# Stick-breaking weights: TensorE's transposes replaced by VectorE's block transposes and a reorder through DRAM, with all heads in one list

## The chip, the cores and the metric

The kernel runs on one core of a Trainium2 chip. The metric is the device time of one execution in microseconds. Before the change it is 520.65 us (median of 3 runs, 520.26 to 520.73). The traces are of one execution taken by the hardware profiler.

## What is computed

One decoder layer over 1,024 tokens of width 1,024. An RMS norm is followed by an input projection into eight parts; three groups (a causal pooling mixer, stick-breaking attention, softmax attention into 256 memory tokens) each get a SiLU gate, and an output projection with a residual follows. The change is in the stick-breaking group, which has 8 heads of width 64:

```python
z = jnp.einsum('bqhd,bkhd->bhqk', qb, kb) * scale      # 128 queries, all keys up to them
mask = s_idx[None, :] < t_idx[:, None]
log_beta = jax.nn.log_sigmoid(z)
log_1m_beta = jnp.where(mask, jax.nn.log_sigmoid(-z), 0.0)
cum = jnp.cumsum(log_1m_beta, axis=-1)
log_a = log_beta + cum[..., -1:] - cum
a = jnp.where(mask, jnp.exp(log_a), 0.0)
out = jnp.einsum('bhqk,bkhd->bqhd', a, vb)
```

All inputs are float32. The kernel keeps that precision by splitting an operand of TensorE into a high part (rounded to the format that TensorE reads) and a low part (what the rounding left), and by adding up the products of the parts.

## The kernel before, in words

The hidden state lies transposed in SBUF as eight high and eight low tiles (`hh`, `hl`). A *unit* of the input projection makes 128 output columns for all tokens, in two halves of 512; a half is eight *steps* of three matmuls of 128x512 (L219, L222). A unit's weights are loaded by SP into the one buffer `wr` (L150), copied to the high part by ScalarE (L161) and subtracted to the low part by GpSimd in four pieces (L165). They are asked for one unit ahead. `u_q`, `u_k`, `u_v`, `u_g` are the units of the stick-breaking heads, two heads (a *pair*) in each; there are four pairs.

The weights `a` are not made by logarithms. `sb_main` takes the sigmoid of minus z (ScalarE, L668) into a tile `be` of 128 queries by L keys, and one scan on VectorE (L672) multiplies these up from the newest key to the oldest. The weights are the differences of neighbours in the scan's result. The kernel takes these differences on V's side instead: `v_unit` subtracts neighbouring rows of V, and the product of the scan's result less one with these differences is the output.

A *group* is one head h of a pair with one j of 0 to 3, that is two blocks of 128 queries (2j and 2j+1). A group has j+1 *chunks* of 256 keys. For each chunk TensorE transposes four 128x128 blocks of `be` (three in the last chunk, whose fourth lies above the diagonal) into PSUM (`a_t`, L517), ScalarE copies them, less one, to `ah` (L522), VectorE makes the low part `al` (L523), and TensorE multiplies V by both (`a_v`, L536). After the last chunk `av_out` adds the two halves of the accumulator, and the gate is multiplied on.

`v_unit` needs V with the tokens in the partitions. It does that already in the way that the change gives to the weights: VectorE transposes each 32x32 block of a 128x512 tile (L316), four DMAs write the blocks to DRAM in pieces of 128 bytes (L320), and two DMAs read them back (L324), after they have landed.

The order of TensorE's work is written by hand. `weave` puts the *main* list (scores, transposes and products of a pair) together with the *fill* list (steps of the projections), so that a main step comes when a simple model of the other engines (`occ`, `lat`) holds it ready. The other engines' orders follow from the order in which the program gives out the work and from what waits for what. All DMAs are issued by SP, one after the other: an issue that waits holds back those behind it. Four `be` tiles and two of each of `ah` and `al` are in turn. After the last pair, one more unit (`u_mg`) and the output projection (seven products, with sums of operands made on VectorE and GpSimd) follow.

## Time and profile before

| | |
|---|---|
| median of 3 runs | 520.65 us (520.26 to 520.73) |
| the profiled execution | 520.78 us, span 519.0 us |
| TensorE clock granted | 1.0 throughout |
| DMA queue of SP | 62,552 packets, 40.98 MB, 27.2% of the 16 engines' span |
| packets under 512 bytes | 27,334 |
| first and last scores of a stick-breaking head | 137.9 and 407.3 us |
| first matmul of the output projection | 438.3 us |

In a row of a group of instructions stand the line, the engine, the operation, what is written from what, the shape and the count; then the busy time in us and the mean in ns of one; then the engine's idle time ahead of them and what ended it. In the chain of waits a row is a start, the time that the piece adds to the end, the engine, the tile and the line. In the timeline a row is a start, a duration, and the instruction.

### The profile page before, as it was taken

The numbers are of one execution on the slowest core, as the hardware profiler recorded it, in microseconds if no ns is written. First come the engines' busy times: TensorE is split into PE (matmuls) and PEld (weight loads), VectorE is DVE, ScalarE is ACT, GpSimd is POOL, SyncE is SP. The second block draws the span as 40 slices with busy tenths as digits, with TensorE's granted clock in tenths as the row PEclk, the third lists the DMA queues.
The fourth block names the chain that finished last, engine by engine and source line by source line (L and its number), as shares of the span: only waits on it lengthen the run. The fifth ranks groups of instructions, "written<-read, shape, count | busy, mean of one in ns | idle before, by whom it ended". The sixth has DMA issues, their size and how long they took to land.

```text
span 519.0 us, 7552 instructions
## 1 busy us (share of the span) xinstructions
PE 506.7 (98%) x2692; PEld 426.1 (82%) x2692; DVE 391.2 (75%) x635; ACT 289.1 (56%) x562; POOL 177.8 (34%) x198
## 2 busy tenths in 40 slices
PE   7889999999999999999999999999999999999997
PEld 6668878888888888888888888888788888888886
DVE  4776776787597876887748776658987769999863
ACT  6887647677666654645455655444635549452400
POOL 4580334465222102202230221132527900045990
PEclk9999999999999999999999999999999999999999
DMA  8911021432311131023401133411010425504033
GB/s 301 352 43 42 3 80 40 104 81 56 88 40 42 42 81 42 1 81 81 101 21 42 42 85 69 92 42 33 9 40 11 153 72 173 169 33 163 0 122 122
DMA packets 62589, 41.45 MB, mean 80 GB/s; under 512 B 27334, under 2 KB 52184, under 8 KB 62552
## 3 DMA queue, kind: packets, MB, share of 16 engines
q1 hardware_dynamic: 62552, 40.98, 27.2%
q8 instruction: 21, 0.34, 0.3%
q14 instruction: 16, 0.13, 0.1%
HBM read 30.48 MB, written 6.29 MB: 71 GB/s over the span
## 4 chain that ended last, share of the span: by engine, by line
PE 88%; ACT 5%; DVE 4%; DMA 1%; issue 1%; SPq 0%; ACTq 0%
PE av L536 8%; PE z L664 7%; PE ta L517 6%; PE u_v L222 6%; PE u_q L222 6%; PE u_g L222 5%; PE u_k L222 5%; PE u_q L219 3%; PE u_v L219 3%; PE u_mg L222 3%; PE oS L1071 3%; PE oS L1073 3%; PE u_pv L222 3%; PE oS L1072 3%; PE u_g L219 3%; PE u_k L219 3%
## 5 line engine op out<-in xcount | busy, mean ns | idle before, releaser
L672 DVE TENSOR_TENSOR_SCAN be<-be,later 128x128 f32<-128x128 f32 (+3 forms) x64 | 92.7, 1462 | 11.9 <-ACT be L668 11.0
L522 ACT ACTIVATE ah<-ta,mone 128x512 fp32r<-128x512 f32 (+1 forms) x80 | 51.3, 644 | 48.7 <-PE ta L517 47.9
L523 DVE SCALAR_TENSOR_TENSOR al<-ta,ah 128x512 fp32r<-128x512 f32 (+1 forms) x80 | 50.4, 632 | 26.8 <-ACT ah L522 26.0
L668 ACT ACTIVATE be<-z 128x128 f32<-128x128 f32 (+3 forms) x96 | 45.6, 490 | 32.5 <-PE z L664 30.1
L517 PE MATMUL ta<-ident,be 128*128 128x128 f32 x288 | 44.8, 273 | 0.0
L517 PEld LDWEIGHTS ta<-ident,be 128*128 128x128 f32 x288 | 35.0, 140 | 7.8 <-DVE be L672 0.6
L536 PEld LDWEIGHTS av<-ah,V_v 128*128 128x128 f32 x160 | 29.7, 188 | 6.7
L536 PE MATMUL av<-al,V_v 128*128 128x256 f32 (+1 forms) x160 | 31.9, 281 | 1.1 <-DVE al L523 1.1
L536 PE MATMUL av<-ah,V_v 128*128 128x256 f32 (+1 forms) x160 | 30.3, 271 | 0.0
L219 PE MATMUL u_g<-hh,wh_g 128*128 128x512 f32 x64 | 27.5, 430 | 0.0
L219 PE MATMUL u_v<-hh,wh_v 128*128 128x512 f32 x64 | 26.7, 417 | 0.0
L219 PE MATMUL u_k<-hh,wh_k 128*128 128x512 f32 x64 | 26.6, 416 | 0.0
L165 POOL TENSOR_TENSOR wl_g<-wr_g,wh_g 128x256 fp32r<-128x256 f32 x16 | 11.3, 738 | 43.9 <-ACT wh_g L161 30.2
L619 POOL TENSOR_SCALAR pe_m<-pe_m,nb_m 128x256 f32<-128x256 f32 x16 | 16.7, 1041 | 27.3 <-DVE nb_m L616 21.5
L1071 PE MATMUL oS<-bs,hh 128*128 128x512 f32 (+1 forms) x68 | 25.9, 381 | 0.0
L1073 PE MATMUL oS<-bs,hl 128*128 128x512 f32 (+1 forms) x68 | 25.8, 379 | 0.0
L1072 PE MATMUL oS<-bs,hh 128*128 128x512 f32 (+1 forms) x68 | 25.6, 376 | 0.0
L608 ACT ACTIVATE pe_m<-z_m,nb_m,qsc 128x256 f32<-128x256 f32 x32 | 17.8, 560 | 13.6 <-DVE nb_m L604 13.4
L222 PE MATMUL u_v<-hl,wh_v 128*128 128x512 f32 x64 | 25.3, 395 | 0.0
L222 PE MATMUL u_g<-hl,wh_g 128*128 128x512 f32 x64 | 25.3, 395 | 0.0
L536 PEld LDWEIGHTS av<-al,V_v 128*128 128x128 f32 x160 | 24.1, 189 | 1.4 <-DVE al L523 1.3
L222 PE MATMUL u_k<-hh,wl_k 128*128 128x512 f32 x64 | 25.3, 395 | 0.0
(315 smaller groups left out, 1471.3 us busy)
## 6 DMA issues: line engine op xcount, KB each, us to landing
x<-in_x_dram SPq DMA_DIRECT2D x8, 512.0 KB, 6.2
wr_q<-in_w_in_dram SPq DMA_DIRECT2D x4, 512.0 KB, 4.0
wr_k<-in_w_in_dram SPq DMA_DIRECT2D x4, 512.0 KB, 4.0
wr_v<-in_w_in_dram SPq DMA_DIRECT2D x4, 512.0 KB, 3.6
KA_k<-KA_k SPq DMA_DIRECT2D x8, 256.0 KB, 4.3
KB_k<-KB_k SPq DMA_DIRECT2D x8, 256.0 KB, 3.6
wr_g<-in_w_in_dram SPq DMA_DIRECT2D x4, 512.0 KB, 3.7
vd_v<-vt_v SPq DMA_DIRECT2D x32, 64.0 KB, 2.0
```

Of the source, the lines that this page charges most:

```text
L219: nc.tensor.matmul(pt[:], wh[:, kc], hh[k][:, c], start=(k == 0), stop=False)
L222: nc.tensor.matmul(pt[:], w[:, kc], h[k][:, c], start=False, stop=(k == KD - 1 and n == 1))
L517: nc.tensor.transpose(tp[:, o : o + P], src, ident[:])
L522: nc.scalar.activation(ah[:, :w], tp[:, :w], AF.Identity, bias=mone[:, 0:1])
L523: nc.vector.scalar_tensor_tensor(al[:, :w], tp[:, :w], -1.0, f(ah[:, :w]), op0=ALU.add, op1=ALU.subtract)
L536: nc.tensor.matmul(av[:, 256 - bw : 256], vs[n], part[:, o : o + bw], start=(first and part is ah and n == 0), stop=(last and part is al a ...
L664: nc.tensor.matmul(zp[:, 0:w], q[h][:, tcol], k[h][:, n, s0 : s0 + w], start=(n == 0), stop=(n == 1))
L668: nc.scalar.activation(be[:, s0 : s0 + w], zp[:, 0:w], AF.Sigmoid, scale=-(HD**-0.5))
L672: nc.vector.tensor_tensor_scan(be[:, rev], be[:, rev], mask, 1.0, op0=ALU.mult, op1=ALU.max)
L1071: nc.tensor.matmul(bk[:, c], xh[:, tcol], wh[:, c], start=(n == 0), stop=False)
L1072: nc.tensor.matmul(bk[:, c], xh[:, tcol], wl[:, c], start=False, stop=False)
L1073: nc.tensor.matmul(bk[:, c], xl[:, tcol], wh[:, c], start=False, stop=(n == 3))
```

## The change

What is in it:

- The transposes `a_t` of the stick-breaking weights and the copies out of PSUM are gone. VectorE transposes the 32x32 blocks of a whole `be` tile in place, right behind its scan. Four DMAs, one for each 32 partitions, write the tile in pieces of 128 bytes to a scratch `zd` in DRAM, where the keys are rows and the group's 256 queries columns. For each chunk one DMA reads 256 rows of it back (two for the last chunk of a group).
- The chunk that is read is copied to the high part by ScalarE, and GpSimd subtracts for the low part, in the place where the chunk was read to (`al`, now three buffers).
- The scan's result is no longer reduced by one. Its share is a constant for each block of queries: V's row at the block's end. `v_unit` keeps these (`ends`), and `av_out` adds them as a bias, in two copies instead of one.
- `sb_slots` makes one list of all 32 groups and 80 chunks in place of a list for each pair. The scores of a group are spread over the slots up to four chunks ahead of its first product; each slot e then holds the read of chunk e+2, the split of chunk e+1 and the product of chunk e. The list is cut into four parts for the four calls of `weave`. The last chunks of a pair come in the next part.
- Some tiles of the pooling mixer change places (`us` to KA0, `pl` to V0, its weights into the buffers `vt` and `qa0`), since V0 is in use for longer.

```diff
@@ v_unit
+            for h in range(2):
+                rows, other = slice(h * HD, (h + 1) * HD), slice((1 - h) * HD, (2 - h) * HD)
+                nc.scalar.activation(ends()[other, 4 * th : 4 * th + 4], pt[rows, 127::128], AF.Copy)
@@ av_out
+            for i in range(2):
+                c = slice(i * P, (i + 1) * P)
+                nc.scalar.activation(tmp[rows, c], av[other, c], AF.Identity, bias=ends[other, i : i + 1])
@@ sb_main becomes sb_slots; qk
                 nc.vector.tensor_tensor_scan(t[:, rev], t[:, rev], mask, 1.0, op0=ALU.mult, op1=ALU.max)
+                nc.vector.transpose(t[:, 0:L], t[:, 0:L])
+                if n not in zd:
+                    zd[n] = dram.tile([2 * (j + 1) * P, 2 * P], F32, tag=f"zd{n}", name=f"zd{n}")
+                t = be.pop((n, i))
+                for a in range(4):
+                    q = slice(32 * a, 32 * a + 32)
+                    o = i * P + 32 * a
+                    nc.sync.dma_start(
+                        zd[n][0:L, o : o + 32].rearrange("(b r) c -> r b c", r=32),
+                        t[q, 0:L].rearrange("p (b c) -> p b c", c=32),
+                    )
-        def tr(j, h, b):
...
-            at[j, h, "t", b] = a_t([one, two], f"{p}_{h}_{j}_{b}", True)
+        def rd(e):
+            n, b = chunks[e]
+            j = groups[n][1]
+            t = pool.tile([P, 512], F32R, tag="al", name=f"al_{e}", bufs=3)
+            r0 = 2 * b * P
+            if b < j:
+                nc.sync.dma_start(
+                    f(t[:]).rearrange("p (k c) -> p k c", k=2),
+                    zd[n][r0 : r0 + 2 * P, :].rearrange("(k p) c -> p k c", p=P),
+                )
+            else:
+                nc.sync.dma_start(f(t[:, 0:256]), zd[n][r0 : r0 + P, :])
+                nc.sync.dma_start(f(t[:, 256:384]), zd[n][r0 + P : r0 + 2 * P, P:])
+            at[e] = t
+        def hl(e):
...
+            hi = pool.tile([P, 512], F32R, tag="ah", name=f"ah_{e}", bufs=2)
+            nc.scalar.activation(hi[:, 0:w], f(lo[:, 0:w]), AF.Copy)
+            nc.gpsimd.tensor_tensor(lo[:, 0:w], f(lo[:, 0:w]), f(hi[:, 0:w]), op=ALU.subtract)
@@ the slots
+            start_, stop_ = (first[n - 1] if n else -2) - ahead, first[n] - ahead
...
+                steps.append(Step(0.0, lambda c=c: rd(c), 0.0, 0.0, [("q", chunks[c][0])]))
...
+                steps.append(Step(0.0, lambda c=e + 1: hl(c), 0.5, 2.4, (), ("t", e + 1)))
...
+                steps.append(Step(0.44, lambda c=e: av(c), 0.4, 0.0, [("t", e)]))
...
-    weave(attn(0), fill_0, 4, 1.0)
+    attn = sb_slots()
+    weave(attn[0], fill_0, 4, 1.0)
```

How this moves the work is seen at three places of the engines' orders. In a row stand the line (of the kernel that the row belongs to), the operation, what is written from what, the shape, and a count where rows that are alike follow each other. The digits at a name's end only number the buffers.

The first is SP's order in pair 1 of the change, while V of pair 2 is projected. `zd_2595` is the scratch of group (j=2, h=1) of pair 1, `zd_2730` that of (j=3, h=0); `be_0_7` is the weight tile of head 0 and the query block 7, written in four DMAs of 1,024 pieces; `vd` and `V_v` are the write and the read of V; `wr_q` is the load of the next unit's weights; `al_2775`, `al_2832`, `al_2851` are chunks 0, 1 and 2 of group (j=2, h=1).

```order
L698 DMA al_2775<-zd_2595 128x2x256
L687 DMA zd_2730<-be_0_7_1_2759 32x32x32 x4
L324 DMA vd_v_385<-vt_v_1_2793 32x16x32 x4
L328 DMA V_v_2699<-vd_v_385 128x4x64
L150 DMA wr_q_2810<-in_w_in_dram 128x8x128
L328 DMA V_v_2699<-vd_v_385 128x4x64
L698 DMA al_2832<-zd_2595 128x2x256
L703 DMA al_2851<-zd_2595 128x256
L704 DMA al_2851<-zd_2595 128x128
L687 DMA zd_2863<-be_1_6_1_2840 32x28x32 x4
```

Before, SP has at the same place, where V of pair 2 is projected, only these:

```order
L320 DMA vd_v_387<-vt_v_0_2685 32x16x32 x4
L324 DMA V_v_2695<-vd_v_387 128x4x64
L150 DMA wr_k_2973<-in_w_in_dram 128x8x128
L324 DMA V_v_2695<-vd_v_387 128x4x64
L320 DMA vd_v_387<-vt_v_1_2750 32x16x32 x4
L324 DMA V_v_2695<-vd_v_387 128x4x64 x2
L150 DMA wr_v_3150<-in_w_in_dram 128x8x128
```

So reads on which a product waits now stand behind writes of other groups' weights, behind V's writes and reads, and behind the load of a projection's weights.

The second is GpSimd's order at the same place of the change: `al_2775` and `al_2832` are the subtractions of chunks 0 and 1 of group (j=2, h=1), `wl_q` is the low part of the weights loaded by `wr_q`, `V_v` the low part of V.

```order
L714 TENSOR_TENSOR al_2775<-al_2775,ah_2834 128x512
L309 MEMSET vt_v_0_3436 128x1
L165 TENSOR_TENSOR wl_q_2813<-wr_q_2810,wh_q_2812 128x256 x4
L337 TENSOR_TENSOR V_v_2699<-V_v_2699 128x8x64
L714 TENSOR_TENSOR al_2832<-al_2832,ah_2854 128x512
L714 TENSOR_TENSOR al_2851<-al_2851,ah_2902 128x384
```

Before, no `al` stood on GpSimd; now a chunk's subtraction stands behind a projection's weights.

The third is GpSimd's order at the end of the attention. `al_4564`, `al_4592` and `al_4605` are the last three chunks of all; `b_V` is a sum of operands for the output projection, in the buffer V0, which holds the pooling mixer's `pl` until its last matmuls (`py`) are done; `wl_mg` is the low part of the last unit's weights.

```order
L165 TENSOR_TENSOR wl_mg_4486<-wr_mg_4483,wh_mg_4485 128x256 x4
L714 TENSOR_TENSOR al_4510<-al_4510,ah_4529 128x512
L714 TENSOR_TENSOR al_4526<-al_4526,ah_4557 128x384
L714 TENSOR_TENSOR al_4555<-al_4555,ah_4566 128x512
L1096 TENSOR_TENSOR b_V_4703<-g_g_1563 128x512
L1096 TENSOR_TENSOR b_V_4703<-g_g_2094 128x512
L1096 TENSOR_TENSOR b_V_4703<-g_g_2882 128x512
L1096 TENSOR_TENSOR b_V_4703<-gp 128x512
L714 TENSOR_TENSOR al_4564<-al_4564,ah_4594 128x512
L714 TENSOR_TENSOR al_4592<-al_4592,ah_4608 128x512
L714 TENSOR_TENSOR al_4605<-al_4605,ah_4627 128x384
```

Before, the four sums stood among the pooling mixer's subtractions and the last unit's weights, with no chunk behind them.

159 lines of the change are left out of this document (84 added, 75 removed).

## The prediction

> **What bounds the kernel now.** I read the page first (engines, then its chain), then the busy times of the stretch from the first stick-breaking scores to the last product's start (137.9 to 438.3 us), then the chain piece by piece.
>
> ```profile
> PE 506.7 (98%) x2692; PEld 426.1 (82%) x2692; DVE 391.2 (75%) x635; ACT 289.1 (56%) x562; POOL 177.8 (34%) x198
> PE 88%; ACT 5%; DVE 4%; DMA 1%; issue 1%; SPq 0%; ACTq 0%
> PE av L536 8%; PE z L664 7%; PE ta L517 6%; PE u_v L222 6%; PE u_q L222 6%; PE u_g L222 5%; PE u_k L222 5%; PE u_q L219 3%; PE u_v L219 3%; PE u_mg L222 3%; PE oS L1071 3%; PE oS L1073 3%; PE u_pv L222 3%; PE oS L1072 3%; PE u_g L219 3%; PE u_k L219 3%
> 137.90:438.30 300.40, 299.25 (x1636) 253.64 (x1635) 228.49 (x312) 166.11 (x303) 79.90 (x87) 1.00 0.22 60
> L536 PE MATMUL av<-al,V_v 128*128 128x256 f32 (+1 forms) x160 | 31.9, 281 | 1.1 <-DVE al L523 1.1
> ```
>
> The reader is to see that TensorE carries 88% of the chain, and in the stretch that the change rewrites it is busy 299 of 300 us (the columns are PE, PEld, DVE, ACT, POOL). Before a product with the low halves (`al`) it waited 1.1 us in all 160 of them. So TensorE time taken out of this stretch is time saved, until something else is late. The other four have room as averages: VectorE 228, ScalarE 166, GpSimd 80 of 300, DMA 22%.
>
> **The change part by part.** *Taken from TensorE: the transposes.* Busy times of matmuls overlap, so I take the price from the chain, where each piece is what it adds:
>
> ```profile
> 240.72 0.44 PE ta L517 x4
> 241.15 0.23 PE u_v L219
> 241.39 0.47 PE u_v L222 x2
> 241.85 0.47 PE av L536 x4
> ...
> 243.03 0.46 PE z L664 x2
> ...
> 245.59 0.33 PE ta L517 x3
> ...
> 247.10 0.35 PE z L664 x2
> ```
> ```profile
> L517 PE MATMUL ta<-ident,be 128*128 128x128 f32 x288 | 44.8, 273 | 0.0
> L522 ACT ACTIVATE ah<-ta,mone 128x512 fp32r<-128x512 f32 x48 | 32.9, 686 | 30.7 <-PE ta L517 30.2
> L522 ACT ACTIVATE ah<-ta,mone 128x384 fp32r<-128x384 f32 x32 | 18.6, 581 | 18.0 <-PE ta L517 17.7
> L523 DVE SCALAR_TENSOR_TENSOR al<-ta,ah 128x512 fp32r<-128x512 f32 x48 | 33.0, 688 | 19.5 <-ACT ah L522 19.1
> L523 DVE SCALAR_TENSOR_TENSOR al<-ta,ah 128x384 fp32r<-128x384 f32 x32 | 17.6, 550 | 7.2 <-ACT ah L522 6.9
> L316 DVE STREAM_TRANSPOSE vt_v<-vt_v 128x512 f32<-128x512 f32 x8 | 5.6, 704 | 0.1
> L333 POOL TENSOR_TENSOR V_v<-V_v 128x512 fp32r<-128x512 f32 x8 | 10.3, 1289 | 26.4 <-ACT V_v L332 26.4
> ```
>
> 48 chunks with four transposes at 0.44 and 32 with three at 0.33 make **31.7 us**. TensorE gets nothing new, so with no new wait the span would be 519.0 - 31.7 = 487.3.
>
> *VectorE, ScalarE, GpSimd as totals.* VectorE loses the 80 low halves (33.0 + 17.6 = 50.6 us) and gets 64 block transposes over 36,864 columns: at 704 ns for 512 that is 50.7, even. ScalarE keeps its 80 copies and splits `av_out`'s copy in two; 166 us of 300 leaves room. GpSimd gets the 80 subtractions, 48 at 1.29 and 32 between 0.97 and 1.29: 93 to 103 us on top of 80. All fit on average, so I cost their totals at nothing. The cover is the idle time above; the order is what can take it away.
>
> *The added wait.* Before, the way from scores to product was scores, sigmoid, scan, TensorE's transposes, split. Now it goes through SP's queue twice, and SP works in order. The worst place comes in pairs 1 and 2 (the SP rows in the section on the change). The read of chunk 1 of group (j=2, h=1), `al_2832`, stands behind the four writes of `be_0_7`, four of V, a read of V that waits for those to land, a weight load and a second V read. On GpSimd its subtraction stands behind the four of that same weight load and V's. So its time counts from the end of the scores z_0_7_0:
>
> ```profile
> L668 ACT ACTIVATE be<-z 128x512 f32<-128x512 f32 x48 | 28.6, 597 | 20.1 <-PE z L664 18.2 <-DVE av L551 0.7
> L672 DVE TENSOR_TENSOR_SCAN be<-be,later 128x1024 f32<-128x1024 f32 x8 | 19.4, 2429 | 1.4 <-ACT be L668 1.1
> 100.27 1.99 SPq L320 DMA_DIRECT2D vd_v<-vt_v  x4
> 102.72 1.46 SPq L324 DMA_DIRECT2D V_v<-vd_v  x2
> L161 ACT ACTIVATE wh_q<-wr_q 128x1024 fp32r<-128x1024 f32 x3 | 3.2, 1061 | 1.3 <-PE u_v L222 1.3
> wr_q<-in_w_in_dram SPq DMA_DIRECT2D x4, 512.0 KB, 4.0
> L165 POOL TENSOR_TENSOR wl_q<-wr_q,wh_q 128x256 fp32r<-128x256 f32 x12 | 8.5, 743 | 25.5 <-ACT wh_q L161 17.7 <-DMA vd_v<-vt_v 7.8
> b_qa<-in_w_out_dram SPq DMA_DIRECT2D x4, 256.0 KB, 2.8
> V_v<-vd_v SPq DMA_DIRECT2D x16, 128.0 KB, 2.2
> L1040 ACT ACTIVATE bs<-b_KA 128x512 fp32r<-128x512 f32 x12 | 7.4, 627 | 6.2 <-PE oA L1073 2.3 <-PE oS L1073 2.1 <-DVE b_KA L1047 1.4
> ```
>
> Three prices are not in the trace. The block transpose of 1024 columns costs between 0.70 (one of 512) and 1.41 (two); I take 1.41. Four writes of 128 KB cost between 1.99, if four issues of V's kind (64 KB each) take that whatever they hold, and 3.98, if it goes by the count of 128-byte pieces. I take 3.98: V's issues lengthen while earlier pieces are still moving. The read of 256 KB lands after 2.2 (128 KB of V) to 2.8 (256 KB of `b_qa`); I take 2.8, the same size.
>
> Sum for this place: sigmoid 0.60, scan 2.43, transpose 1.41, writes 3.98, V's writes 1.99: 10.41. V's read starts 0.46 after them (102.72 - 100.27 - 1.99), and I count 0.38 for its issue: 11.25, when the weight load issues. It lands 4.0 later and is copied in 1.06: 16.3. GpSimd: four subtractions of 743 ns, V's 1.29, then the chunk's 1.29: **21.9 us**. The data itself would be there earlier, so the load sets it. Meanwhile TensorE has, counted in its order and priced by the chain's pieces, 12 steps of a projection (0.70 each), three chunks' products (0.47 each), and scores of 0.35, 0.46 and 0.46: 11.1 us. It waits **10.8 us**. With the low ends of transpose and writes it is 8.1.
>
> The second place recurs in all four pairs. The read of chunk 2 of group (j=3, h=0) stands on SP behind the writes of `be_1_7`. From z_1_7_0: 0.60 + 2.43 + 1.41 + 3.98 + 2.8 + copy 0.63 + subtraction 1.29 = 13.1 (low ends 9.9). TensorE's work between, counted likewise: pair 0 6.7, pair 1 10.2, pair 2 12.3, pair 3 9.0 (there a weight load stands between too, 0.4). Waits: 6.4, 2.9, 0.8, 4.5. In pairs 0 and 3 the first place has no V in it and also costs 13.1, against 10.4 and 11.8: waits 2.7 and 1.3.
>
> The third place is the end, on GpSimd (the last order rows): four subtractions for the output projection stand ahead of the last three chunks', and they need a buffer that py, 5.4 us before the planned last products, frees.
>
> ```profile
> L1143 POOL TENSOR_TENSOR xr<-xr,b_V 128x512 f32<-128x512 f32 x4 | 6.0, 1522 | 0.0
> ```
>
> Four at 1.52 and three at 1.29 are 9.97 after py. The last chunk's products start then instead of 5.4 after it: 4.6 us late.
>
> Sum of waits: pair 0 9.1, pair 1 13.7, pair 2 11.6, pair 3 10.4 with the end: **44.8 us** (by all low ends some 25). 519.0 - 31.7 + 44.8 = 532.1. The profiled execution took 520.78, 1.78 more than its span, and lies 0.13 above the median of 520.65. So **534** is forecast, with 514 to 534 between the unknown prices alone.
>
> **A rule of the Trainium skill.** GpSimd's new subtractions have two inputs in SBUF, and so has the scan:
>
> ```profile
> 302.78 1.76 DVE L672 TENSOR_TENSOR_SCAN be<-be,later 128x768 f32<-128x768 f32 x1 [0.76 <-ACT be L668]
> 371.81 5.15 DVE L672 TENSOR_TENSOR_SCAN be<-be,later 128x768 f32<-128x768 f32 x2
> ```
> ```profile
> L672 DVE TENSOR_TENSOR_SCAN be<-be,later 128x640 f32<-128x640 f32 x8 | 13.3, 1668 | 0.6 <-ACT be L668 0.4
> ```
> ```profile
> 369.95 1.29 POOL L781 TENSOR_TENSOR pl<-us,ph 64x512 fp32r<-64x512 f32 x1 [1.63 <-ACT ph L780]
> 371.31 1.62 POOL L781 TENSOR_TENSOR pl<-ps,ph 64x512 fp32r<-64x512 f32 x1
> 373.00 2.62 POOL L781 TENSOR_TENSOR pl<-us,ph 64x512 fp32r<-64x512 f32 x1
> ```
>
> Alone, a scan of 768 took 1.76; one of 768 and one of 640 in a row (1.67 on average) beside GpSimd's subtractions took 5.15, and a subtraction of 1.29 became 2.62. The Trainium skill, "GPSIMD Engine Reference", § 8 Key points, says that GpSimd shares its SBUF interfaces with VectorE and contends with VectorE instructions that have two SBUF inputs; by that rule the trace agrees. It speaks against putting the subtractions on GpSimd; it is the second rival below.
>
> **The rivals.**
> 1. *TensorE stays the bound; faster.* For it: the averages, and that all writes of a tile but the last leave early. If all three low ends hold and the weight load does not hold GpSimd, the first place takes 0.60 + 2.43 + 0.70 + 1.99 + 1.99 + 0.46 + 1.46 (V's reads), 0.37 for issuing the load, 2.2 to land and 1.92 for copy and subtraction: 14.1 (waits of 3.0 in pairs 1 and 2); the second waits 3.2 in pair 0 and 1.3 in pair 3, the end 4.6: 15 in all, so 519.0 - 31.7 + 15 + 1.8 = **504**. Full cover would give 489. Against it: SP's order is fixed, and a read cannot pass a write that waits.
> 2. *VectorE and GpSimd in each other's way; slower.* The place is the two late chains of each pair, eight in all. Each meets one scan, longer by (5.15 - 1.76 - 1.67) / 2 = 0.9, and one subtraction, longer by 1.3. 8 x 2.2 = 18 more: **552**. It decides as soon as subtractions and scans overlap mostly, and GpSimd at 177 of 300 us makes that likely; against it, most of my waits have idle engines.
> 3. *The change gives back just what it takes*: 25 to 33 us of waits, within 0.2%. Nothing favours this but the low ends.
>
> That the transposes do not leave TensorE is excluded: its order has 256 rows fewer (2021 against 2277).
>
> **How the numbers follow.** The forecast, waits of 33 to 52 us (522 to 541): 0.46, slower. Rival 1, 489 to 519: 0.33, faster. Rival 2, 541 and more: 0.13, slower. Rival 3: 0.08. Slower 0.59, same 0.08, faster 0.33, where 0.2% is about what a measurement of this kernel can tell from no change. The range leaves out 0.1 at the fast end and 0.07 at the slow end: 500 to 554. The forecast's own range is 522 to 541.
>
> **What would show it.** Right: no `ta`; TensorE no longer busy all through, its idle time in a few gaps of 3 to 11 us per pair, ahead of `av`, released by GpSimd's `al`; the longest two in pairs 1 and 2 ahead of chunk 1 of (j=2, h=1); SP waiting for the block transpose, with the reads issued right behind the writes. Wrong: TensorE busy throughout and a span near 488 to 505; four writes of `be_0_7` issued within 2 us; reads landed long before their products. For rival 2: scans of 1024 well over 2.43 and subtractions well over 1.29.

## The result and the profile after

| | before | after |
|---|---|---|
| median of 4 runs | 520.63 us (520.26 to 520.73) | 678.52 us (676.54 to 679.83) |
| ratio, 95% interval | | 1.303 (1.299 to 1.307) |
| span of the profiled execution | 519.0 us | 678.1 us |
| mean granted TensorE clock | 1.00 | 0.90 |

The change makes the kernel 30% slower. The sign was forecast, the size was not: 534 us, in a range of 500 to 554.

The page of the changed kernel: its busy times, the granted clock in 40 slices (tenths), and the shares of the chain that ended last.

```profile
PE 546.4 (81%) x2404; PEld 436.1 (64%) x2404; DVE 400.6 (59%) x619; ACT 293.4 (43%) x610; POOL 286.0 (42%) x277
...
PEclk9979999997969898978799878699776877799999
...
PE 36%; issue 22%; POOL 15%; DMA 8%; DVE 8%; ACT 6%; SPq 4%; POOLq 0%; DVEq 0%; ACTq 0%
```

TensorE was 12.3 us idle before (519.0 - 506.7) and is 131.7 us idle now. Its busy time grew by 39.7 us, though 288 transposes of it are gone: the clock, full throughout before, now dips in most slices. So the 159.1 us of longer span are 119.4 us of waiting and 39.7 us of busy time; if the transposes took 31.7 us with them, the slower clock made TensorE's work some 71 us longer (an estimate; from the mean clock, if TensorE had work all through the slow stretches: 0.101 x 678.1 = 68). The waits of the changed kernel, longest first in total (us, times, longest):

```profile
POOL al L714 <- ACT ah L713: 150.1, 36, 10.7
ACT be L675 <- PE z L671: 133.6, 57, 7.3
...
PE av L532 <- POOL al L714: 80.7, 56, 4.3
...
PE av L532 <- ACT ah L713: 37.9, 32, 3.2
```

TensorE waits for the split weights at most chunks, 118.6 us in all, never long (4.3 us at most). Where before all 160 products with `al` waited 1.1 us, each chunk now waits 1.5 us on average, and 54 of the 80 chunks wait over 0.3 us. What holds the split up is seen in the idle time ahead of its instructions (groups by shape; behind the second bar the idle time just before them and what ended it):

```profile
L713 ACT ACTIVATE ah<-al 128x512 fp32r<-128x512 f32 x48 | 29.5, 622 | 11.2 <-PE av L532 5.3 <-POOL al L714 3.2 <-DMA al<-zd 2.5
L713 ACT ACTIVATE ah<-al 128x384 fp32r<-128x384 f32 x32 | 16.5, 515 | 2.1 <-DMA al<-zd 2.0
L714 POOL TENSOR_TENSOR al<-al,ah 128x512 fp32r<-128x512 f32 x48 | 68.0, 1422 | 103.1 <-ACT ah L713 103.1
```

This is the row that matters: the 80 copies `ah` together waited 4.5 us (2.5 + 2.0) for their own read to land. ScalarE has 57% of idle time, yet when it comes to a copy, the data has long been there. One chunk in the timeline (start, duration, instruction, and in brackets the idle time before), ScalarE first, then SP and TensorE:

```profile
261.87 0.50 ACT L713 ACTIVATE ah<-al 128x384 fp32r<-128x384 f32 x1
267.67 0.62 ACT L550 ACTIVATE avt<-av,ve_v 64x128 f32<-64x128 f32 x2 [5.30 <-PE av L532]
269.30 0.28 ACT L675 ACTIVATE be<-z 128x128 f32<-128x128 f32 x1 [1.01 <-PE z L671]
271.37 0.60 ACT L675 ACTIVATE be<-z 128x512 f32<-128x512 f32 x1 [1.79 <-PE z L671]
272.76 0.59 ACT L293 ACTIVATE KA_k<-u_k 64x512 fp32r<-64x512 f32 x1 [0.79 <-PE u_k L222]
273.37 0.59 ACT L293 ACTIVATE KB_k<-u_k 64x512 fp32r<-64x512 f32 x1
273.98 0.63 ACT L713 ACTIVATE ah<-al 128x512 fp32r<-128x512 f32 x1
```
```profile
261.18 0.54 SPq L698 DMA_DIRECT2D al<-zd  x1
```
```profile
274.67 0.50 PE L532 MATMUL av<-ah,V_v 128*128 128x256 f32 x2 [1.24 <-ACT ah L713]
276.01 0.51 PE L532 MATMUL av<-al,V_v 128*128 128x256 f32 x2 [0.85 <-POOL al L714]
```

The read went out at 261.2; such reads land after 3.1 us (median). The copy ran at 274.0. In between ScalarE stood idle for 8.9 us, waiting for TensorE: the order put the copy behind a bias, two sigmoids and the two copies of `u_k`, whose matmuls TensorE had only just done. TensorE then waited for the copy, and for GpSimd behind it. It is a loop: TensorE waits for ScalarE, which waits for what TensorE made a moment ago.

GpSimd's order holds TensorE up as well. The first 5.3 us of ScalarE's idle time above are of this kind. The copy of 261.87 was done at 262.4, but on GpSimd its subtraction stood behind four pieces of a projection's weights:

```profile
262.04 4.14 POOL L165 TENSOR_TENSOR wl_v<-wr_v,wh_v 128x256 fp32r<-128x256 f32 x4 [3.22 <-ACT wh_v L161]
266.14 0.99 POOL L714 TENSOR_TENSOR al<-al,ah 128x384 fp32r<-128x384 f32 x1
```
```profile
267.19 0.45 PE L532 MATMUL av<-al,V_v 128*128 128x256 f32 x2 [4.31 <-POOL al L714]
```

By the times of the single instructions, 46 of the 80.7 us of waiting for `al`, at 22 chunks, passed while the copy was done and GpSimd was still at earlier instructions.

### The profile page after: what moved, and what is told of

It reads as the page before. It is cut to its first block, busy times and chain, and to the rows that moved or that the text cites. A ratio compares the mean times of both kernels' runs of the same rounds, so it can differ in the third digit from the quotient of the medians.

```text
span 678.1 us, 8025 instructions
## 1 busy us (share of the span) xinstructions
PE 546.4 (81%) x2404; PEld 436.1 (64%) x2404; DVE 400.6 (59%) x619; ACT 293.4 (43%) x610; POOL 286.0 (42%) x277
## 4 chain that ended last, share of the span: by engine, by line
PE 36%; issue 22%; POOL 15%; DMA 8%; DVE 8%; ACT 6%; SPq 4%; POOLq 0%; DVEq 0%; ACTq 0%
POOL al L714 8%; SPq L687 3%; PE av L532 3%; DVE be L679 3%; PE u_v L222 3%; PE oS L1120 2%; PE oS L1122 2%; PE oS L1121 2%; DMA al<-zd 2%; PE u_mg L222 2%; DMA zd<-be 2%; PE oA L1120 2%; PE oA L1122 2%; PE oA L1121 2%; PE u_q L222 2%
## 5 line engine op out<-in xcount | busy, mean ns | idle before, releaser
L714 POOL TENSOR_TENSOR al<-al,ah 128x512 fp32r<-128x512 f32 (+1 forms) x80 | 104.2, 1314 | 158.4 <-ACT ah L713 150.1
L532 PE MATMUL av<-al,V_v 128*128 128x256 f32 (+1 forms) x160 | 41.5, 346 | 80.7 <-POOL al L714 80.7
L552 DVE TENSOR_TENSOR av<-av,avt 64x256 f32<-64x256 f32 x32 | 13.9, 434 | 67.4 <-ACT avt L550 67.1
L550 ACT ACTIVATE avt<-av,ve_v 64x128 f32<-64x128 f32 x64 | 19.8, 357 | 72.6 <-PE av L532 72.4
L680 DVE STREAM_TRANSPOSE be<-be 128x128 f32<-128x128 f32 (+3 forms) x64 | 49.6, 776 | 1.9
L713 ACT ACTIVATE ah<-al 128x512 fp32r<-128x512 f32 (+1 forms) x80 | 44.8, 579 | 13.3 <-PE av L532 5.3
L671 PE MATMUL z<-KB_k,qb_q 128*128 128x512 f32 (+3 forms) x96 | 30.2, 408 | 0.2 <-ACT be L675 0.2
L671 PE MATMUL z<-KA_k,qa_q 128*128 128x512 f32 (+3 forms) x96 | 27.8, 400 | 0.0
L222 PE MATMUL u_g<-hh,wl_g 128*128 128x512 f32 x64 | 27.6, 432 | 0.0
L222 PE MATMUL u_k<-hl,wh_k 128*128 128x512 f32 x64 | 27.0, 422 | 0.0
```

The lines of the kernel that those rows point to most:

```text
L222: nc.tensor.matmul(pt[:], w[:, kc], h[k][:, c], start=False, stop=(k == KD - 1 and n == 1))
L532: nc.tensor.matmul(av[:, 256 - bw : 256], vs[n], part[:, o : o + bw], start=(first and part is ah and n == 0), stop=(last and part is al a ...
L671: nc.tensor.matmul(zp[:, 0:w], q[h][:, tcol], k[h][:, m, s0 : s0 + w], start=(m == 0), stop=(m == 1))
L680: nc.vector.transpose(t[:, 0:L], t[:, 0:L])
L713: nc.scalar.activation(hi[:, 0:w], f(lo[:, 0:w]), AF.Copy)
L714: nc.gpsimd.tensor_tensor(lo[:, 0:w], f(lo[:, 0:w]), f(hi[:, 0:w]), op=ALU.subtract)
```

## The experiments

Times are one run each beside a run of the kernel before (520.4 to 521.2 us), except where an interval is given. From run to run the first scores came at 137.7 to 139.7 or at 140.6 to 142.7 us, whatever was tried, so that differences of up to 5 us between single runs say nothing. In all seven of the later starts TensorE waited 3.7 us for `x` until about 40 us, instead of 1.8 or less in all others but one, and in six of them the clock was halved for 3.4 or 6.8 us behind that.

Behind each run I also counted, in the order of its instructions, how short each copy `ah` comes: on ScalarE, the latest TensorE result that anything ahead of the copy needs; from there the TensorE work up to the copy's product, by the chain's prices (0.23 us for 512 columns). Evacuating the result (0.6), the copy (0.6) and the low half (1.3) need 2.5 us; what is missing is the *shortfall*. The changed kernel has it at 46 of 80 copies, 70 us together. Waits of ScalarE for a DMA, and the orders of the other engines, are not in this count.

### First four: the read's place on SP, and the clock

**old_reads**: pairs 1 to 3 read what pair 0 wrote (the other two reads of `rd` alike).

```diff
-  nc.sync.dma_start(f(t[:, 0:256]), zd[n][r0 : r0 + P, :])
+  nc.sync.dma_start(f(t[:, 0:256]), zd[n % 8][r0 : r0 + P, :])
```

> In pairs 1 to 3 every read fetches the weights that pair 0 wrote at the same place, so it no longer waits for writes of its own pair to land; the products of pairs 1 to 3 are therefore made with pair 0's weights. Theory A (order in SP's queue): the read still stands on SP behind the writes of the step before, and these still wait for VectorE, so little changes: 655 to 680 us, products of pairs 1 to 3 still 5 us or more apart per chunk. Rival B (the way through DRAM is too long: a read waits for its own data): pairs 1 to 3 lose that wait and come to 3.3 to 4 us a chunk, 560 to 610 us in all.

671.1 us, as theory A had it. The orders of all engines are those of the changed kernel, so nothing else moved. That a read waits for the writes of its own pair to land is not what bounds this kernel; rival B fell.

**no_writes**: the same, and for pairs 1 to 3 no DMAs behind the block transposes.

```diff
   nc.vector.transpose(t[:, 0:L], t[:, 0:L])
+  if p > 0:
+      be.pop((n, i))
+      return
```

> As the run with pair 0's weights, and pairs 1 to 3 write nothing to DRAM (the block transposes stay). Theory A: with no waiting write ahead of the reads on SP, pairs 1 to 3 run at TensorE's own pace, 3.3 to 3.7 us a chunk, pair 0 stays at 4.8: 540 to 570 us, and the granted clock of pairs 1 to 3 is near 1. Rival D (ScalarE's or GpSimd's order holds the chunks up, or the three buffers of al): still 4.5 us a chunk or more, 610 us or more.

591.0 us, between the two. Without the writes more than half of the loss goes, but 40 us of waits ahead of products stay.

**reads_on_act** (the other two reads alike):

```diff
-  nc.sync.dma_start(f(t[:, 0:256]), zd[n][r0 : r0 + P, :])
+  nc.scalar.dma_start(f(t[:, 0:256]), zd[n][r0 : r0 + P, :])
```

> Nothing is left out: the reads of the weights are issued by ScalarE instead of SP, so that no write stands ahead of them. Theory A: what held them up is gone in all four pairs; 500 to 535 us, waits ahead of the products from 119 us to under 40. Rival D (the wait only moves: ScalarE now waits for the product that frees the buffer, and all sigmoids and copies behind it wait too): 600 us or more, with ScalarE idle ahead of the reads' successors.

644.9 us, a time as rival D had it. The waits ahead of the products fell to 46.7 us, near what A wanted, but the time did not follow. SP now stands still between its writes. Below are a stretch of its queue in this run, the longest of its waits (us in total, times, longest), and the issues of all writes in this run and in the changed kernel (minimum, median and maximum in ns):

```profile
321.71 22.14 SPq L687 DMA_DIRECT2D zd<-be  x24
```
```profile
SPq L687 <- DMA al<-zd: 110.2, 41, 11.3
```
```profile
L687 SPq DMA_DIRECT2D zd<-be x256: 302/469/2577, 142.8 to 525.0; - x128
L687 SPq DMA_DIRECT2D zd<-be x256: 302/477/2307, 144.5 to 558.4; - x128
```

The first row runs from the start of the first of 24 writes to the end of the last. The issues themselves are no slower than before (0.47 us against 0.48); some 10 of the 22 us are issue, and the rest is waiting, part of it for block transposes. In all, SP waited 110 us ahead of its writes for reads of `al` to land. No write needs a read. But the program gives its DMAs, whichever engine issues them, eight semaphores in turn, and a DMA waits until the one that had its semaphore before has landed. So SP's writes came to wait for reads that stand in ScalarE's order. The weight loads stand behind these writes on SP, and TensorE waits for `wh` (9.3 us ahead of `u_pv`, 7.5 ahead of `u_q`, none before).

**busy_six**

```diff
+  dm = ps("tr", f"dm_{e}")
+  for i in range(6):
+      nc.tensor.matmul(dm[:], hh[i][:, 0:P], hh[i][:, 0:512], start=True, stop=True)
   a_v(acc[n], [v[:, 2 * b, h, :], v[:, 2 * b + 1, h, :]], at.pop(e), b == 0, b == j)
```

> Ahead of each chunk's products TensorE gets six more matmuls of 512 columns whose results nobody reads (1.4 us a chunk at full clock, 112 us in all), to keep its clock up while it would wait. Theory C (the halved clock is a cause of its own, 70 us): the clock stays near 1 and the time falls to 640 us or less in spite of the added work. Theory A: the time is set by the queue, the added work fills waits; 665 to 710 us with a clock near 1, and waits ahead of the products cut by about half or more.

684.0 us at a mean clock of 0.96, in theory A's range.

```profile
PE 614.8 (90%) x2884; PEld 502.5 (74%) x2884; DVE 400.3 (59%) x619; ACT 292.4 (43%) x610; POOL 277.2 (41%) x277
```

480 added matmuls of 0.232 us are 111 us; TensorE's own work is then 503 us, 43 less than in the changed kernel, and its waits for `av` are 53.9 instead of 118.6. The time is 5 us longer: some 65 us of the added work went into waits, and 43 us were paid by the faster clock. Theory C's range fell. But the run does not tell what the slower clock costs by itself, since the added work took up what the clock gave back.

### Four more: pieces, GpSimd, the list

**long_pieces** and **long_pieces_act**, the second with the reads on ScalarE as above:

```diff
-  zd[n][0:L, o : o + 32].rearrange("(b r) c -> r b c", r=32),
-  t[q, 0:L].rearrange("p (b c) -> p b c", c=32),
+  zd[n][:].rearrange("a c -> (a c)")[o * L - i * P * P : o * L - i * P * P + 32 * L].rearrange("(p l) -> p l", p=32),
+  t[q, 0:L],
...
-  zd[n][r0 + P : r0 + 2 * P, P:]
+  zd[n][r0 + P - 64 : r0 + 2 * P - 64, P:]
```

> The writes keep their number, their bytes and their waits, but each row of a write goes to DRAM as one piece (512 bytes to 4 KB) instead of pieces of 128 bytes; the blocks are then not reordered, so the products are made with weights in the wrong places, and the last read of a group fetches rows that lie 64 higher. Theory A (order: reads behind writes that wait for VectorE, on SP): the waits stay, 650 to 680 us. Rival E (the DMA engines' time for the small pieces, 40 us of issue in every 100 where they are queued): 560 to 620 us.

> As the run with long pieces, with the reads issued by ScalarE. If order and small pieces each hold a part (A and E together): SP is no longer behind, four writes take about 2 us of issue instead of 4.3, 530 to 575 us. If only the order counted: 630 to 645 us, as with reads on ScalarE alone. If both are beside the point (rival D, the queues of ScalarE and GpSimd): 600 us or more.

636.9 us, between the two, and 585.1 us, 10 above the first range. Together the two edits take off more (93 us) than one by one (42 and 34). A write took 0.42 us of issue instead of 0.48 (medians), so small pieces as such cost SP little.

**low_on_dve**

```diff
-  nc.gpsimd.tensor_tensor(lo[:, 0:w], f(lo[:, 0:w]), f(hi[:, 0:w]), op=ALU.subtract)
+  nc.vector.tensor_tensor(lo[:, 0:w], f(lo[:, 0:w]), f(hi[:, 0:w]), op=ALU.subtract)
```

> The low halves are computed by VectorE instead of GpSimd; nothing is left out. Theory A: the products wait as long for a late read whoever subtracts, 655 to 690 us, with the 81 us that TensorE waits for GpSimd's al now put down to VectorE's. Rival F (GpSimd's own order: the subtraction stands behind the low halves of the weights): most of the 81 us goes, 590 to 630 us.

647.4 us, outside both. A subtraction of 512 columns took 0.79 us instead of 1.42; 61 of the 81 us of waiting for `al` stayed, now put down to VectorE. GpSimd was slower. Its order is not cleared by this: 53 of the 61 us, at 40 chunks, passed while the copy was done and VectorE was still at earlier instructions (46 us on GpSimd in the changed kernel). The edit put the subtraction from one full queue into another.

**list_with_pe**: the new list, with `a_t` instead of transpose, writes, reads and split, and

```diff
-  ahead = 4
+  ahead = 1
```

> Only the one list of all heads with the V ends added by ScalarE: TensorE's transposes stay as before, no block transposes, no DRAM, scores one chunk ahead instead of four, since the tiles of be are then held until they are transposed. If the list itself costs nothing: 515 to 530 us. Rival (the list puts the fill work or a pair's first scores in the wrong places): 540 us or more.

532.3 us, between the two, 11 above before; the start took 4.7 of them (first scores at 142.6 us), four waits of TensorE's transposes for the scan another 4.7. The list, with scores one chunk ahead, is a small part of the loss.

### All of it out at once, and a small part alone

**act_and_dve** is reads_on_act and low_on_dve together, **act_dve_long** adds long_pieces, **nothing_late** is no_writes with both.

> Reads issued by ScalarE and low halves on VectorE, both at once; nothing is left out. Alone these took off 34 and 31 us. If each shortens a part of one way that sets the time, they add: 605 to 625 us. If they cover the same wait, only one counts: 635 to 655 us.

> The same with long pieces besides (each row of a write as one piece, blocks not reordered, so the products are made with weights in the wrong places). Long pieces with reads on ScalarE took 585 us. If the three parts add: 540 to 565 us. If VectorE, which then has the scan, the block transposes and the subtractions, becomes the bound: 575 us or more.

> Pairs 1 to 3 write nothing to DRAM and read the weights of pair 0 (their products are made with those), reads are issued by ScalarE and low halves computed by VectorE. If the way through the queues was the whole cause, TensorE is the bound again in pairs 1 to 3: 3.3 to 3.6 us a chunk, 525 to 550 us in all with pair 0 still slow, and a granted clock of 0.97 or more in the stretch of these pairs. If TensorE's own order or the fill work around it costs time too: 4 us a chunk or more, 565 us or more.

630.2 us, 573.6 us (both a little above their first range: the parts do not simply add) and 553.5 us, 3.5 above the range; in pairs 1 and 2 it came true. The stretches of nothing_late from a pair's first product to the next pair's (columns PE, PEld, DVE, ACT, POOL, clock, DMA share, GB/s), and below them pairs 1 and 2 of the kernel before:

```profile
154.30:243.80 89.50, 71.38 (x303) 56.24 (x302) 62.72 (x81) 39.44 (x78) 14.56 (x16) 0.85 0.61 138
243.80:310.00 66.20, 64.38 (x322) 53.22 (x321) 63.09 (x83) 39.86 (x83) 20.03 (x21) 1.00 0.52 134
310.00:376.70 66.70, 65.86 (x331) 54.76 (x330) 63.91 (x88) 39.30 (x83) 23.18 (x22) 1.00 0.54 141
376.70:457.50 80.80, 62.27 (x273) 49.15 (x272) 74.23 (x97) 35.96 (x71) 35.40 (x26) 0.90 0.35 111
```
```profile
208.80:279.50 70.70, 70.70 (x394) 60.29 (x393) 50.19 (x67) 38.53 (x71) 14.37 (x21) 1.00 0.25 60
279.50:351.60 72.10, 72.10 (x400) 61.57 (x399) 50.65 (x70) 38.09 (x70) 14.31 (x20) 1.00 0.25 59
```

Pairs 1 and 2 take 66.2 and 66.7 us, 3.3 a chunk, at full clock with TensorE busy nearly throughout; before they took 70.7 and 72.1. With no writes, the reads on ScalarE and the low halves on VectorE the block transposes do what they were put in for. Pair 0, which still writes, takes 89.5; in pair 3 VectorE, with everything on it, is busy for 74 of 81.

**one_chunk_dram**: the kernel before, with the new way for one chunk of ten in each head (behind the transpose four writes as in the change; `rd` reads them back into a tile of its own, `hl` copies them less one and subtracts on VectorE; to make room, `avt` has one buffer instead of two, and small tiles of the pooling mixer share others).

```diff
   nc.vector.tensor_tensor_scan(be[:, rev], be[:, rev], mask, 1.0, op0=ALU.mult, op1=ALU.max)
+  if j == 3:
+      nc.vector.transpose(be[:, 768:L], be[:, 768:L])
...
+  if j == 3 and b == 2:
+      steps.append(Step(0.0, lambda h=h: rd(h), 0.0, 0.0, [("q", n)]))
+  if j == 3 and b == 3:
+      steps.append(Step(0.0, lambda h=h: hl(h), 0.65, 1.9, [("q", n)], ("t", n, b)))
+  else:
       steps.append(Step(0.43, lambda j=j, h=h, b=b: tr(j, h, b), 0.65, 1.9, [("q", n)], ("t", n, b)))
```

> The kernel before, with only the last chunk of the two longest groups of each pair (j=3, b=3) taken through block transposes and DRAM: 8 chunks of 80, 24 transposes. There the weights have some three chunks of TensorE's work (11 us) between the last scores and the products, about as much as the way needs. If it stays covered, TensorE loses 8 x 0.33 = 2.6 us: 517.5 to 519 us, ratio 0.994 to 0.997. If the way is late even there: 521 us or more, with waits ahead of the product released by ah or al.

528.26 us, ratio 1.014 (1.012 to 1.016). TensorE waited at two of the eight places, the first head of pairs 1 and 2:

```profile
PE av L536 <- ACT ah_d L695: 5.8, 2, 3.2
```
```profile
255.89 1.93 SPq L320 DMA_DIRECT2D vd_v<-vt_v  x4
258.29 0.38 SPq L324 DMA_DIRECT2D V_v<-vd_v  x1
258.77 0.94 SPq L680 DMA_DIRECT2D zd<-be  x2
259.82 0.40 SPq L324 DMA_DIRECT2D V_v<-vd_v  x1
260.26 0.99 SPq L680 DMA_DIRECT2D zd<-be  x2
261.30 0.45 SPq L688 DMA_DIRECT2D ad<-zd  x1
```

There the last writes share SP with V's, and TensorE is ready for the product at 261.9, before the read has landed. Each of these waits also halved the clock for the next 3.4 us.

### Where the reads and scores stand

The prediction had waits at three places; the cause of those at all other chunks was open.

**lead_four** (the mask's tile also holds the identity, to make room), **scores_eight** (second diff), and **lead_all**, which is lead_four with act_and_dve:

```diff
-  t = pool.tile([P, 512], F32R, tag="al", name=f"al_{e}", bufs=3)
+  t = pool.tile([P, 512], F32R, tag="al", name=f"al_{e}", bufs=4)
-  if 0 <= e + 2 < len(chunks):
-      c = e + 2
+  if 0 <= e + 3 < len(chunks):
+      c = e + 3
...
-  tmp = pool.tile([P, 256], F32, tag="avt", name=f"avt_{name}", bufs=1)
+  tmp = slot("be", f"avt_{name}")[:, 0:256]
```
```diff
-  ahead = 4
+  ahead = 8
```

> Reads are issued one chunk earlier, into four buffers of al instead of three (the room comes from the copy of the product's halves, which now takes a tile of be for a moment, and from the identity, which shares the mask's tile). If the three-chunk lead of the reads sets the period: one chunk more, some 3.5 to 5 us, goes into every read's way, 600 to 645 us. If the reads' issue is bound by the queue itself, whatever their lead: 660 to 690 us.

> Scores run eight chunks ahead of the products instead of four; nothing is left out. If it is the scores that come too late for the products: under 620 us. If the reads' place in SP's queue sets it (each still stands behind the writes of the step before it, whichever group these belong to): 660 to 690 us.

> Four buffers and reads one chunk earlier, reads issued by ScalarE, low halves on VectorE; nothing is left out. Without the fourth buffer this took 630 us. If lead and queues add: 580 to 610 us. If the DMA engines' time for the small pieces is what is left: 615 to 640 us.

692.6 us (above either range), 670.6 and 624.7 us (each in its second). Earlier reads made it worse, earlier scores changed next to nothing. The theory of the lead fell, and why it could not help shows in lead_four: the copies waited 1.6 us for their reads, all 80 together.

```profile
L713 ACT ACTIVATE ah<-al 128x512 fp32r<-128x512 f32 x48 | 28.5, 622 | 2.8 <-POOL al L714 2.4 <-DMA al<-zd 0.3
L713 ACT ACTIVATE ah<-al 128x384 fp32r<-128x384 f32 x32 | 16.6, 518 | 3.2 <-POOL al L714 1.7 <-DMA al<-zd 1.3
```

**six_places**: one_chunk_dram without the two places that waited.

```diff
-  if j == 3:
+  if j == 3 and (h or p in (0, 3)):
```

> As one_chunk_dram, without the two places that waited there (first head of pairs 1 and 2): six chunks of 80 by block transposes and DRAM, 18 of TensorE's 288 transposes. If they stay covered: TensorE loses 6 x 0.33 = 2.0 us and nothing waits, 518 to 519.5 us, ratio 0.995 to 0.998. If the added DMAs and VectorE work cost something elsewhere: 520.5 us or more.

529.97 us, ratio 1.016 (1.014 to 1.019): no gain either. Waits of 1.7 us for `ah_d` appeared at two other places (the second head of pairs 1 and 2), the clock was halved for 3.4 us behind one of them, and the start was slower (first scores at 141.3 us, 3.4 later). Eighteen transposes are worth 2.0 us by the chain's prices; the two late chunks took 3.3 us of waits.

### ScalarE's order

**act_hand**: ScalarE keeps the order in which the program gives out its work, as TensorE does already.

```diff
+  hand = ExitStack()
+  hand.enter_context(tc.manual_schedule(engines={mybir.EngineType.Activation}))
   attn = sb_slots()
...
+  hand.close()
   mixed = [g() for g in gp] + [sb[p][3][0]() for p in range(4)] + y_mem
```

**act_hand_lead_eight** adds lead_four and scores_eight.

> In the attention part ScalarE keeps the order in which its instructions are written (TensorE's is kept so already); SP, VectorE and GpSimd are still ordered by the scheduler, and TensorE's order is the same instruction for instruction. Counted in the order of the changed kernel: 46 of 80 copies ah stand on ScalarE behind the evacuation of a TensorE result that is less than 2.5 us of TensorE work ahead of their product (evacuation 0.6, copy 0.6, low half 1.3), together 70 us short; written order: 2 copies, 2 us short. Theory G (ScalarE's order holds up the products): 600 to 645 us, waits ahead of the products from 119 us to 70 or less. If the reads, SP or GpSimd's subtraction set the time: 660 us or more.

> ScalarE's order as written, and besides four buffers of al with reads one chunk earlier and scores eight chunks ahead, which by themselves gave 692.6 and 670.6 us. If these did nothing only because ScalarE's order was the tighter limit: clearly below act_hand, 580 to 620 us. If SP's queue (writes and reads in order) or the DMA engines are the next limit whatever the lead: as act_hand within 10 us.

640.9 and 631.6 us. The order of ScalarE around one copy, in the changed kernel and in act_hand (it is the copy of the timeline above; the numbers of buffers are two higher in act_hand, and a row can stand for two instructions):

```
238 L675 ACTIVATE be_1_4_1_2581<-z_1_4_0_2589 128x512
239 L293 ACTIVATE KA_k_2490<-u_k_1_2519 64x512
240 L293 ACTIVATE KB_k_2491<-u_k_1_2519 64x512
241 L713 ACTIVATE ah_2541<-al_2498 128x512
```
```
234 L675 ACTIVATE be_0_5_1_2541<-z_0_5_1_2538 128x256
235 L713 ACTIVATE ah_2543<-al_2500 128x512
236 L675 ACTIVATE be_0_5_1_2541<-z_0_5_0_2546 128x512
```

The copy moves ahead of seven instructions. In act_hand:

```profile
L713 ACT ACTIVATE ah<-al 128x512 fp32r<-128x512 f32 x48 | 30.2, 628 | 75.1 <-DMA al<-zd 69.5 <-PE z L671 5.1
L713 ACT ACTIVATE ah<-al 128x384 fp32r<-128x384 f32 x32 | 16.7, 522 | 62.8 <-DMA al<-zd 41.0 <-PE av L532 8.3 <-PE z L671 6.7
...
PE 35%; DMA 15%; DVE 13%; SPq 12%; issue 9%; ACT 8%; POOL 7%; DVEq 0%; ACTq 0%; POOLq 0%
```

The waits ahead of the products fell from 118.6 to 64.3 us, and what the copies wait for turned over: 110 us for the data instead of 4.5. DMA and SP's queue rose from 12% to 27% of the chain. So ScalarE's order was a limit, the edit is worth 38 us, and the way through SP and DRAM is a second one right behind it; that is why old_reads and lead_four had found nothing. The 38 us are not ScalarE's order alone. TensorE's order is the same instruction for instruction, but the scheduler ordered the other three anew: some 70 of SP's 528 instructions, 90 of VectorE's 619 and 40 of GpSimd's 274 stand elsewhere, and the waits for `al` behind earlier work of GpSimd fell from 46 to 16 us.

With this order, lead and distance take off 9 us where they had cost 14 and gained 8, although the copies hardly wait for reads there (21.8 us). What holds the products up in that run is the written order itself: ScalarE waits 84 us for weights of projections (39.6, 18.1, 16.9 and 9.0 us ahead of `wh_g`, `wh_pg`, `wh_k` and `wh_mg`), which SP asks for late, and copies stand right behind:

```profile
353.83 1.06 ACT L162 ACTIVATE wh_g<-wr_g 128x1024 fp32r<-128x1024 f32 x1 [13.94 <-DMA wr_g<-in_w_in_dram]
```

The runs side by side, by the two limits (waits ahead of the products; idle time of the copies until their own read landed):

| | time | shortfall on ScalarE | waits of `av` | copies wait for reads |
|---|---|---|---|---|
| lead_four | 692.6 | 94 us at 55 | 109.2 | 1.6 |
| busy_six (with the added matmuls) | 684.0 | 18 at 27 | 53.9 | 2.4 |
| the change | 678.5 | 70 at 46 | 118.6 | 4.5 |
| old_reads | 671.1 | 70 at 46 | 115.6 | 4.6 |
| scores_eight | 670.6 | 65 at 43 | 115.1 | 0 |
| low_on_dve | 647.4 | 68 at 44 | 99.5 | 3.9 |
| long_pieces | 636.9 | 59 at 40 | 96.9 | 3.9 |
| reads_on_act | 644.9 | 20 at 13 | 46.7 | 37.2 |
| act_hand | 640.9 | 2 at 2 | 64.3 | 110.4 |
| act_and_dve | 630.2 | 20 at 13 | 38.9 | 46.2 |
| act_hand_lead_eight | 631.6 | 7 at 5 | 86.7 | 21.8 |
| lead_all | 624.7 | 39 at 27 | 52.5 | 38.9 |
| no_writes | 591.0 | 26 at 16 | 39.6 | 47.4 |
| long_pieces_act | 585.1 | 4 at 4 | 16.3 | 45.4 |
| act_dve_long | 573.6 | 6 at 5 | 10.6 | 32.7 |
| nothing_late | 553.5 | 9 at 6 | 13.9 | 32.3 |

The copies of the upper seven hardly ever wait for a read; the others do. In busy_six the shortfall is small because the added matmuls stand in the gap. The table also shows what the experiments could not keep apart: whatever is edited, the scheduler orders ScalarE anew (old_reads alone kept every order). Long pieces and reads on ScalarE changed the order of the copies too, so their 42 and 34 us are not the price of small pieces, or of SP's queue, alone; and the eight semaphores tie the queues of both engines together.

## Why the prediction was wrong

1. *The gain.* -31.7 us on TensorE was somewhat high. Pair 1 of nothing_late has the same 322 other matmuls as before, at full clock, and TensorE is busy for 64.4 us in it instead of 70.7: 72 transposes were worth 6.3 us there, some 25 in all four pairs (by pair 2, some 28).
2. *The cover.* GpSimd's total rose by 108 us (93 to 103 forecast), VectorE's by 9, and no engine ran out of time. But the sentence "the order is what can take it away" was then followed up for SP and GpSimd only, at eleven chunks. **This is the step that failed: the other 69 chunks were taken as covered, their copies as run when their data was there, and ScalarE's order was not read.** In its place the runs showed 119 us of waits instead of 45, 90 of them at those 69 chunks. ScalarE's order put 46 copies too late; that was there to be counted before the run, 70 us of shortfall, more than all the waits of the forecast. GpSimd's order, which was read, also held TensorE up at chunks that were left out: 36 of the 46 us. Giving ScalarE its written order, with the reordering of other engines that came with it, took off 38 us. How the rest divides among the queues is open.
3. *The prices.* The block transpose of 1024 columns took 1.25 (1.41 taken), four writes of such a tile 2.25 (3.98 taken), the read of 256 KB landed after 3.1 (2.8 taken):

```profile
303.19 1.25 DVE L680 STREAM_TRANSPOSE be<-be 128x1024 f32<-128x1024 f32 x1
```
```profile
304.52 2.25 SPq L687 DMA_DIRECT2D zd<-be  x4
```
```profile
al<-zd SPq DMA_DIRECT2D x48, 256.0 KB, 3.1
```

4. *The places.* The mechanism was there. At the first place in pair 1:

```profile
319.69 0.80 PE L532 MATMUL av<-ah,V_v 128*128 128x256 f32 x2 [2.81 <-ACT ah L713]
323.94 0.79 PE L532 MATMUL av<-al,V_v 128*128 128x256 f32 x2 [3.46 <-POOL al L714]
```
```profile
318.67 2.77 POOL L165 TENSOR_TENSOR wl_q<-wr_q,wh_q 128x256 fp32r<-128x256 f32 x4 [7.70 <-DMA zd<-be]
321.40 1.26 POOL L337 TENSOR_TENSOR V_v<-V_v 128x512 fp32r<-128x512 f32 x1
322.62 2.22 POOL L714 TENSOR_TENSOR al<-al,ah 128x512 fp32r<-128x512 f32 x2
```

   GpSimd does the weight load's four and V's one ahead of the chunk, as foretold; the wait is 6.3 us, the longest chunk's of pairs 1 and 2, not 10.8, since four writes take 1.7 us less and TensorE, late elsewhere, comes later. In pairs 0 and 3 it is 1.8 and 2.2 (2.7 and 1.3 forecast). The second place waits 2.7, 1.1, 1.3 and 4.8 us (6.4, 2.9, 0.8, 4.5), the end 2.7 (4.6). Together that is 29 us of the 45. The other 90 us lie at chunks that the forecast counted as covered. By the 29 alone the span would be 516 us with a gain of 31.7 and 523 with one of 25, against 519.0 before: near no change. That the sign came out right so clearly is due to waits and a clock that the forecast did not have; to that extent it was luck.
5. *Waits as a sum.* They were added up as if each stood alone. But a wait of TensorE delays the results that ScalarE's next instructions need, and these stand ahead of the next copy.
6. *The clock* was put at nothing, without a reason, and this failed too: in the sum it weighs as much as what the forecast lacked in waits: 519.0 - 31.7 + 119.4 of idle time + 71.4 of longer busy time = 678.1. It is no cause apart from the waits, since each fall follows a window in which TensorE waited (last section). What the time would be at full clock no run shows.
7. *Rival 2* (VectorE and GpSimd in each other's way) had its scans slower; those of 1024 columns took 2.29 us against 2.43 before. GpSimd's subtraction did get slower, 1.42 us on average instead of 1.29, and VectorE doing it instead took off 31 us. *Rival 1* holds where nothing is late (66 us a pair). Its bounds and those of rival 3 overlap: 25 to 33 us of waits are 514 to 522 us, and only 31 to 33 lie within 0.2%. The low ends of the second place add up to 9.8, not 9.9. Neither moves the forecast.

```profile
L679 DVE TENSOR_TENSOR_SCAN be<-be,later 128x1024 f32<-128x1024 f32 x8 | 18.3, 2292 | 55.8 <-ACT be L675 54.0 <-DMA wr_mg<-in_w_in_dram 1.9
```

What stays open: how the loss divides among the orders of ScalarE, GpSimd, VectorE and SP, the eight semaphores and the DMA engines' time; what the slower clock costs by itself; and why `x` comes later in some runs. No version tried beats the kernel before.

## What to carry to other kernels

Room in an engine's total says nothing about its order: for each new instruction, look at what stands ahead of it on its engine and when TensorE makes what that needs. When one wait is cured and nothing moves, look which idle time took its place; the row of idle time ahead of the instruction says whether it waited for its data or for its turn. Work is worth moving off the busiest engine only if the detour's latency is covered at every place, since in one_chunk_dram two late chunks cost 5.8 us of waits, and the transposes of a chunk are worth 0.3 to 0.4. And a timeline row that stands for many issues runs from the first to the last: what lies between them may be waiting, not their price.

## What the runs showed of the hardware

*The clock halves on half-busy windows.* Four neighbouring windows of 3.4 us in the changed kernel:

```profile
260.80:264.20 3.40, 1.83 (x8) 1.06 (x7) 3.30 (x5) 1.55 (x3) 2.16 (x2) 1.00 0.95 220
264.20:267.60 3.40, 0.41 (x3) 0.41 (x4) 0.43 (x1) 0.00 (x0) 2.93 (x4) 1.00 1.00 180
267.60:271.00 3.40, 3.40 (x11) 2.73 (x11) 0.87 (x2) 0.90 (x3) 0.00 (x0) 0.50 0.75 153
271.00:274.40 3.40, 2.43 (x11) 1.62 (x9) 2.34 (x2) 2.20 (x4) 0.00 (x0) 1.00 0.00 0
```

A window with 0.41 us of TensorE work is followed by one at half clock, that one, fully busy, by full clock. The window of the first row, busy for 54%, kept the clock. All 23 falls in this trace follow a window in which TensorE was busy for at most 51%, and during the attention each return one with 86% or more; a half-clock window of 84% did not bring it back. The limit is about one half, not a sharp one: in lead_four a window of 55% lost the clock, and one of 49% kept it. The Trainium skill, "TensorE: Matmul & The Clock Gate", Part 1, has the same two states and the same window (about 3.4 us), and ties the fall to an idle window. The length agrees. No window need be idle: 21 of the 23 were not, and the one with 51% had no gap over 1.5 us.

*Small pieces cost little at the issue.* A write in pieces of 128 bytes took 0.48 us of issue (median of 256) in the changed kernel, and 0.42 in long_pieces, where a piece has 512 bytes or more. The Trainium skill, "DMA: Bandwidth & Descriptors", section "Issuing engines are not separate DMA queues", says that a second issuing engine only saves issue time, as all run on the same 16 DMA engines. Nothing here speaks against it, and no run tests it alone: in reads_on_act a write of SP took as long to issue (0.47) and 2.2 us to land (mean of the medians of the eight sizes; 2.1 in the changed kernel), but SP waited for reads by the program's semaphores.
